# Hybrid token mixer: the input projection's three matmuls per weight tile become a 512-column and a 256-column one, with the halves added outside PSUM

## The chip, the cores and the metric

The kernel runs on 1 core of one Trainium2 chip. The metric is the device time of one execution in microseconds; the kernel before was timed in three runs, and their median is 1374.41 us (1373.37 to 1375.53). The engines of the core run side by side, each through its own list of instructions in a fixed order: TensorE (PE) does matmuls and loads their weights, VectorE (DVE) and ScalarE (ACT) do elementwise work, SyncE (SP) starts the weight transfers. PSUM is the memory that PE writes and that ACT and DVE read; everything else lies in SBUF.

## The reference

One layer on 256 tokens of width 2048. One input projection makes the inputs of three token mixers (Mamba-2 SSD, S5, RWKV-7), of their gates, and of three merge gates.

```python
proj = jnp.einsum('bsd,dc->bsc', x, w_in[l])          # 2048 -> 18592 columns
z_a, xbc, dt_raw, u_b, z_b, p_rkvz, p_w, p_a, p_gate = jnp.split(proj, offs, axis=-1)
y_a = mamba2_branch(z_a, xbc, dt_raw, ...)            # convolution over 4 tokens, SSD in chunks of 128
y_b = s5_branch(u_b, z_b, ...)                        # complex diagonal recurrence, GLU
y_c = rwkv7_branch(p_rkvz, p_w, p_a, ...)             # recurrence with 64x64 states, 16 heads
gates = jax.nn.sigmoid(p_gate.reshape(b, s, N_BRANCHES, d) + gate_b[l])
merged = (gates[:, :, 0] * (y_a @ w_branch_a[l]) + gates[:, :, 1] * (y_b @ w_branch_b[l])
          + gates[:, :, 2] * (y_c @ w_branch_c[l]))
x = layer_norm(DEEPNORM_ALPHA * x + merged @ w_out[l], ln_g[l], ln_b[l])
```

## The kernel before

Every large product is kept accurate by splitting both operands into a high and a low part of a rounded type (fp32r) and adding three products: high by high, high by low, low by high. The projection goes tile by tile, 128 output columns at a time, 145 tiles: 48 of the merge gates (`g0`, `g1`, `g2`), 32 of `x` (the input of the SSD convolution), 16 of `za`, 8 each of `z`, `v`, `u`, `r`, `k`, `zb`, and one `lora`. The name of a tile is the name of its PSUM tile: `ps_x4`, `ps_za5`.

For one tile `loadw` (L358) fetches 128 columns of weights as two half tiles; ACT makes their high part (L369) and DVE their low part (L371). Rings of four half tiles each (`raw`, `hi`, `lo`) let these run ahead of PE by two tiles. `proj` (L377) then issues, for each of 16 blocks of 128 input channels, three matmuls of 256 columns (the tokens): weights high by `xhi` (L381), weights high by `xlo` (L382), weights low by `xhi` (L383), 48 in a tile and 6960 in all, into one PSUM tile of a ring of three (tag `pj`). The weights are loaded into PE anew for each matmul. What uses a tile reads it straight from PSUM: the RWKV shift (`rwkv_shift`, ACT L439 and DVE L440) for `r`, `k`, `v`; the SSD convolution (`ssd_group`, one ACT pass L790 and three DVE passes L792) for `x`; a SiLU on ACT (L800) for `za`; a tanh (L512, L1189, L1201) for the gates.

Between these wide matmuls PE has small ones, 32 to 128 columns each, of the recurrences: the inverse of diagonal blocks (`py`, L647 to L655), the RWKV chunks (`ch`, L675 to L699: each chunk is a chain from PE to ACT or DVE and back), the SSD chunks (`st`, `y`, `cb`). Their order among the wide matmuls isn't written out: tables (`PROG` for the RWKV stage, `PROG2` for the rest) give the order of the stages and tiles, and a scheduler, with a model of the engines' times, lays all instructions out into one fixed list per engine; what stands under `high_priority` it draws forward. Engines wait for one another by semaphores. A new tile in a ring waits until the readers of the tile whose place it takes are done: `R` (the shifted `r`, ring of 2), `cv` (convolved tiles and gates of the SSD groups, ring of 11), `pj`.

After the projection tiles come the branch products (L1155 to L1157), the output product (L1257 to L1259, 512 columns) and the layer norm.

## Time and profile before

| | |
|---|---|
| time, median of 3 runs | 1374.41 us |
| span of the profiled execution | 1372.4 us |
| PE busy | 1353.5 us, 99% |
| DVE busy | 964.9 us, 70% |
| ACT busy | 829.1 us, 60% |
| share of the chain of work that ended last on PE | 97% |

Busy is time in which an engine ran something; the span runs from the first to the last recorded event of the profiled execution. The weight loads (PEld) overlap the matmuls. The duration printed for one matmul includes its passage through the array, and so is longer than the step from one matmul to the next: the steps are read from the starts.

### The profile page before, as it was taken

What the parts mean: (1) busy time and instruction counts of PE and PEld (TensorE: products, weight loads), DVE (VectorE), ACT (ScalarE), POOL (GpSimd) and SP (SyncE); (2) the same over time, 40 slices, a digit from 0 to 9 for tenths busy, and PEclk for the clock granted to TensorE, in tenths of its full rate; (3) what the DMA queues carried; (4) which work ended last, traced back from release to release, by engine and by line L of the source; (5) the groups of instructions that cost most, each with busy time, mean ns of one, the idle gap of its engine ahead of it and who ended that gap; (6) DMA issues with size and microseconds to landing.
All of it is one profiled execution on the core that took longest, in us unless ns stands there. A gap on an engine that the chain in (4) does not pass through costs nothing.

```text
span 1372.4 us, 28474 instructions
## 1 busy us (share of the span) xinstructions
PE 1353.5 (99%) x11436; PEld 1268.5 (92%) x11436; DVE 964.9 (70%) x1765; ACT 829.1 (60%) x1507; POOL 7.4 (1%) x54
## 2 busy tenths in 40 slices
PE   7999999999999999999999999999999999999996
PEld 7999989988999899899999999999999999999885
DVE  5658876455866765579999966799776665547755
ACT  5657565567555556887668877676645544444431
POOL 0000000000000000000000000000000000000000
PEclk9999999999999999999999999999999999999998
DMA  8545554433454345456555555555655556668751
GB/s 293 167 130 161 170 156 150 138 110 120 142 152 141 126 147 154 124 159 194 164 173 170 178 172 173 155 168 180 188 176 173 174 184 202 197 209 253 245 179 62
DMA packets 96661, 230.12 MB, mean 168 GB/s; under 512 B 26545, under 2 KB 41233, under 8 KB 96529
## 3 DMA queue, kind: packets, MB, share of 16 engines
q1 hardware_dynamic: 95936, 227.42, 53.9%
q8 instruction: 90, 1.47, 0.4%
q10 hardware_dynamic: 592, 0.89, 0.2%
q14 instruction: 43, 0.34, 0.1%
HBM read 224.00 MB, written 3.21 MB: 166 GB/s over the span
## 4 chain that ended last, share of the span: by engine, by line
PE 97%; ACT 1%; DMA 1%; DVE 1%; issue 0%; SPq 0%; DVEq 0%
PE ps_g L381 7%; PE ps_g L382 7%; PE ps_g L383 7%; PE ps_x L381 5%; PE ps_x L382 5%; PE ps_x L383 5%; PE br L1156 5%; PE br L1155 4%; PE br L1157 4%; PE po L1259 2%; PE po L1257 2%; PE po L1258 2%; PE ps_za L382 2%; PE ps_za L381 2%; PE ps_za L383 2%; PE ps_r L381 1%
## 5 line engine op out<-in xcount | busy, mean ns | idle before, releaser
L381 PE MATMUL ps_g<-xhi,hi_g 128*128 128x256 f32 x768 | 218.5, 284 | 0.0
L382 PE MATMUL ps_g<-xlo,hi_g 128*128 128x256 f32 x768 | 217.9, 284 | 0.0
L383 PE MATMUL ps_g<-xhi,lo_g 128*128 128x256 f32 x768 | 216.9, 282 | 0.0
L371 DVE TENSOR_TENSOR lo_g<-raw_g,hi_g 128x1024 fp32r<-128x1024 f32 x96 | 117.5, 1224 | 74.2 <-ACT hi_g L369 69.6
L369 ACT ACTIVATE hi_g<-raw_g 128x1024 fp32r<-128x1024 f32 x96 | 101.5, 1058 | 110.9 <-PE ps_g L382 81.8
L381 PE MATMUL ps_x<-xhi,hi_x 128*128 128x256 f32 x512 | 147.3, 288 | 0.0
L382 PE MATMUL ps_x<-xlo,hi_x 128*128 128x256 f32 x512 | 147.0, 287 | 0.0
L383 PE MATMUL ps_x<-xhi,lo_x 128*128 128x256 f32 x512 | 146.8, 287 | 0.0
L382 PEld LDWEIGHTS ps_g<-xlo,hi_g 128*128 128x128 f32 x768 | 144.6, 188 | 1.9 <-issue 0.8
L381 PEld LDWEIGHTS ps_g<-xhi,hi_g 128*128 128x128 f32 x768 | 144.6, 188 | 1.7
L383 PEld LDWEIGHTS ps_g<-xhi,lo_g 128*128 128x128 f32 x768 | 144.6, 188 | 0.9 <-issue 0.4
L369 ACT ACTIVATE hi_b<-raw_b 128x1024 fp32r<-128x1024 f32 x64 | 67.8, 1059 | 74.3 <-PE br L1156 42.9
L371 DVE TENSOR_TENSOR lo_x<-raw_x,hi_x 128x1024 fp32r<-128x1024 f32 x64 | 78.2, 1223 | 39.1 <-ACT hi_x L369 38.7
L381 PEld LDWEIGHTS ps_x<-xhi,hi_x 128*128 128x128 f32 x512 | 97.2, 190 | 2.3 <-issue 1.6
L382 PEld LDWEIGHTS ps_x<-xlo,hi_x 128*128 128x128 f32 x512 | 97.2, 190 | 2.1 <-issue 1.1
L383 PEld LDWEIGHTS ps_x<-xhi,lo_x 128*128 128x128 f32 x512 | 97.1, 190 | 1.6 <-issue 1.1
L369 ACT ACTIVATE hi_x<-raw_x 128x1024 fp32r<-128x1024 f32 x64 | 67.5, 1054 | 48.7 <-PE ps_x L382 25.1
L371 DVE TENSOR_TENSOR lo_b<-raw_b,hi_b 128x1024 fp32r<-128x1024 f32 x64 | 78.2, 1222 | 24.5 <-ACT hi_b L369 22.8
L382 PE MATMUL ps_za<-xlo,hi_za 128*128 128x256 f32 x256 | 73.1, 285 | 0.0
L381 PE MATMUL ps_za<-xhi,hi_za 128*128 128x256 f32 x256 | 73.0, 285 | 0.0
L383 PE MATMUL ps_za<-xhi,lo_za 128*128 128x256 f32 x256 | 72.6, 284 | 0.0
L1156 PE MATMUL br<-yh0l,hi_b 128*128 128x256 f32 x256 | 72.3, 283 | 0.0
(441 smaller groups left out, 4075.5 us busy)
## 6 DMA issues: line engine op xcount, KB each, us to landing
raw_g<-in_wt SPq DMA_DIRECT2D x96, 512.0 KB, 3.8
raw_x<-in_wt SPq DMA_DIRECT2D x64, 512.0 KB, 3.7
...
```

The costliest lines, as they stand in the source:

```text
L369: nc.scalar.activation(hi, raw, AF.Copy)
L371: nc.vector.tensor_tensor(lo, raw, hi.bitcast(F32), ALU.subtract)
L381: nc.tensor.matmul(ps, lhsT=hi.k(k), rhs=g.xhi[:, k, :], start=(k == 0), stop=False)
L382: nc.tensor.matmul(ps, lhsT=hi.k(k), rhs=g.xlo[:, k, :], start=False, stop=False)
L383: nc.tensor.matmul(ps, lhsT=lo.k(k), rhs=g.xhi[:, k, :], start=False, stop=(k == NK - 1))
L1155: nc.tensor.matmul(ps, lhsT=hi.k(k0 + k), rhs=h, start=(k == 0), stop=False)
L1156: nc.tensor.matmul(ps, lhsT=hi.k(k0 + k), rhs=l, start=False, stop=False)
L1157: nc.tensor.matmul(ps, lhsT=lo.k(k0 + k), rhs=h, start=False, stop=(k == n - 1))
L1257: nc.tensor.matmul(po, lhsT=m[0][:, t], rhs=hi.k512(k), start=f0, stop=False)
L1258: nc.tensor.matmul(po, lhsT=m[0][:, t], rhs=lo.k512(k), start=False, stop=False)
L1259: nc.tensor.matmul(po, lhsT=m[1][:, t], rhs=hi.k512(k), start=False, stop=l0)
```

## The change

`xhi` and `xlo` become the two halves of one tile `xx`, so that a weight tile's high part can be streamed against both as one matmul of 512 columns. The PSUM tile is twice as wide: its first half gathers high by high, its second half high by low and then, from a 256-column matmul, low by high. There are two matmuls for each block, 4640 in all, where there were three, and two loads of weights. At the end of a tile ACT copies the second half into SBUF and DVE adds the first half to it, both drawn forward by priority. What used PSUM before now reads that sum. The sum goes into a new ring of two (`pjs`) or, for `g2`, `za`, `zb` and the other gates, into the tile that the next step works on anyway. The ring `pj` keeps three buffers.

```diff
-    g.xhi = g.xf.tile([128, NK, T], F32R, name="xhi")
-    g.xlo = g.xf.tile([128, NK, T], F32R, name="xlo")
+    g.xx = g.xf.tile([128, NK, 2, T], F32R, name="xx")
+    g.xhi, g.xlo = g.xx[:, :, 0, :], g.xx[:, :, 1, :]
...
+        g.pjs = lambda nm: g.rp.tile([128, T], F32, nm, "pjs", 2)
...
+        g.pjs = lambda nm: kp.tile([128, T], F32, name=nm, tag="pjs", bufs=2)
...
-    def proj(n):
+    def proj(n, out=None):
         hi, lo = loadw(I["wt"][TIDX[n]], n, parts=4 if n in ("lora", "k0", "k1") else 1)
-        ps = g.pp.tile([128, T], F32, name="ps_" + n, tag="pj", bufs=3)
+        ps = g.pp.tile([128, 2, T], F32, name="ps_" + n, tag="pj", bufs=3)
         for k in range(NK):
-            nc.tensor.matmul(ps, lhsT=hi.k(k), rhs=g.xhi[:, k, :], start=(k == 0), stop=False)
-            nc.tensor.matmul(ps, lhsT=hi.k(k), rhs=g.xlo[:, k, :], start=False, stop=False)
-            nc.tensor.matmul(ps, lhsT=lo.k(k), rhs=g.xhi[:, k, :], start=False, stop=(k == NK - 1))
-        return ps
+            nc.tensor.matmul(ps, lhsT=hi.k(k), rhs=g.xx[:, k, :, :], start=(k == 0), stop=False)
+            nc.tensor.matmul(ps[:, 1, :], lhsT=lo.k(k), rhs=g.xhi[:, k, :], start=False, stop=(k == NK - 1))
+        with tc.high_priority():
+            s = g.pjs("pj_" + n) if out is None else out
+            nc.scalar.activation(s, ps[:, 1, :], AF.Copy)
+            nc.vector.tensor_tensor(s, ps[:, 0, :], s, ALU.add)
+        return s
...
-        ps = g.proj(f"za{2 * gr + q}")
         z = g.cv(f"zs{q}_{gr}")
+        ps = g.proj(f"za{2 * gr + q}", z)
         with tc.high_priority():
             nc.scalar.activation(z, ps, AF.Silu)
```

The scheduler lays the instructions out anew. The wide tiles keep their order on PE; the small matmuls move against them. Two places matter below. In the kernel after, the two wide matmuls are L384 (512 columns) and L385 (256), and the copy and the add are L388 (ACT) and L389 (DVE); other lines after `proj` stand six further down.

**From `za4` to `za5` (SSD stage).** On PE before, the small matmuls `y0` (SSD group 0), `ch6`, `ch7` (RWKV chunks of heads 6 and 7) stood in groups inside projection tiles, here inside `ps_x4`:

```order
L381 MATMUL ps_x4_7170<-xhi_69,hi_x4_0_7160 128x256
L852 MATMUL y0_6645<-csb1_0_6604,xdt0_6619 64x128 x2
L856 MATMUL y0_6645<-Cd0_6630,ST0_6628 64x128 x2
L852 MATMUL y0_6645<-csb0_0_6602,xdt0_6619 64x128 x2
L852 MATMUL y0_6645<-csb1_0_6604,xdt0_6619 64x128
L680 MATMUL ch7_1_5360<-X7_1_5365,TTf3_3764 64x64 x2
L680 MATMUL ch6_2_5382<-X6_2_5387,TTf3_3764 64x64 x2
L852 MATMUL y0_6645<-csb1_0_6604,xdt0_6619 64x128
L856 MATMUL y0_6645<-Cd0_6630,ST0_6628 64x128 x2
L382 MATMUL ps_x4_7170<-xlo_70,hi_x4_0_7160 128x256
```

Their neighbours on PE now begin where `ps_za4` ends:

```order
L385 MATMUL ps_za4_6469<-xx_69,lo_za4_1_6467 128x256
L384 MATMUL ps_za4_6469<-xx_69,hi_za4_1_6465 128x512
L385 MATMUL ps_za4_6469<-xx_69,lo_za4_1_6467 128x256
L661 MATMUL py3_0_4542<-TTf3_3302,Yl3_0_4543 32x32 x4
L686 MATMUL ch6_0_4655<-X6_0_4658,TTf3_3302 64x64 x2
L681 MATMUL ch7_0_4671<-SVA7_3660,XS7_3642 64x64 x2
L653 MATMUL py3_1_4574<-cst_167,TTf3_3302 32x32 x4
L693 MATMUL ch6_0_4655<-SVA6_3458,bkT6_3459 64x64 x2
L657 MATMUL py3_1_4574<-Yl3_1_4575,Aoff3_3301 32x32 x4
L703 MATMUL ch6_0_4655<-MTr6_3483,SVA6_3458 64x64 x2
```

and end where `ps_za5` begins, 45 rows (87 matmuls) later, with no wide matmul among them:

```order
L681 MATMUL ch7_2_4753<-SVA7_3660,XS7_3642 64x64 x2
L858 MATMUL y0_5807<-csb1_0_5766,xdt0_5781 64x128 x2
L862 MATMUL y0_5807<-Cd0_5792,ST0_5790 64x128 x2
L858 MATMUL y0_5807<-csb0_0_5764,xdt0_5781 64x128 x2
L858 MATMUL y0_5807<-csb1_0_5766,xdt0_5781 64x128 x2
L862 MATMUL y0_5807<-Cd0_5792,ST0_5790 64x128 x2
L681 MATMUL ch6_3_4775<-SVA6_3458,XS6_3440 64x64 x2
L686 MATMUL ch7_2_4753<-X7_2_4758,TTf3_3302 64x64 x2
L384 MATMUL ps_za5_6518<-xx_69,hi_za5_0_6508 128x512
L385 MATMUL ps_za5_6518<-xx_69,lo_za5_0_6510 128x256
```

So the small matmuls of some 23 groups now form one block between two tiles. `ps_za5` takes the PSUM buffer of `ps_x18`, and so waits until that has been copied and added. On ACT before, the convolution of `x4` (`xs0_2`) stood ahead of the chunk's next copies, and read PSUM:

```order
L677 ACTIVATE X7_2_5409<-ch7_2_5404 128x64
L369 ACTIVATE hi_x18_1_7300<-raw_x18_1_7298 128x1024
L790 ACTIVATE xs0_2_7219<-ps_x4_7170,par_166 128x256
L677 ACTIVATE X6_3_5431<-ch6_3_5426 128x64
L683 ACTIVATE SVA7_4174<-ch7_2_5404 64x64 x2
L817 ACTIVATE BT1_7085<-cb1_7081 128x128
L683 ACTIVATE SVA6_3946<-ch6_3_5426 64x64 x2
```

On ACT now it stands behind the decay factors (`csb`, `Cd`) of SSD groups 0 and 1, and the copy of `ps_x18` nine rows behind it:

```order
L689 ACTIVATE SVA7_3660<-ch7_1_4709 64x64 x2
L796 ACTIVATE xs0_2_6288<-pj_x4_6285,par_165 128x256
L689 ACTIVATE SVA6_3458<-ch6_2_4731 64x64 x2
L851 ACTIVATE csb1_0_5766<-csb1_0_5766 128x512
L851 ACTIVATE csb0_1_6159<-csb0_1_6159 128x512
L677 ACTIVATE SVA7_3660<-S7_1_4722 64x64 x2
L699 ACTIVATE SW7_2_4767<-S7_1_4722,W47_3636 128x64
L677 ACTIVATE SVA6_3458<-S6_2_4744 64x64 x2
L706 ACTIVATE XS7_3642<-ch7_1_4709 128x64
L706 ACTIVATE XS6_3440<-ch6_2_4731 128x64
L388 ACTIVATE pj_x18_6393<-ps_x18_6360 128x256
L799 ACT_TABLE_LOAD
```

The copy `pj_x18` writes the `pjs` slot that `pj_x4` held, which `xs0_2` reads; `xs0_2` writes a `cv` slot that DVE's product of `Cd0` with the tile `C_0` frees.

**From `u3` to `g2_13` (RWKV stage).** On PE before, the block inverse of batch 1 (`py1`) began inside `ps_r6`:

```order
L383 MATMUL ps_k7_3700<-xhi_69,lo_k7_1_3698 128x256
L715 MATMUL rlb0_2193<-rhl_229,selT_227 128x256
L715 MATMUL rlb1_2198<-rhl_229,selT_227 128x256
L647 MATMUL py1_0_2282<-cst_168,TTf1_1044 32x32 x4
L381 MATMUL ps_r6_3780<-xhi_69,hi_r6_0_3770 128x256
L382 MATMUL ps_r6_3780<-xlo_70,hi_r6_0_3770 128x256
```

On PE now its matmuls follow the end of `ps_u3`:

```order
L384 MATMUL ps_u3_3722<-xx_69,hi_u3_1_3718 128x512
L385 MATMUL ps_u3_3722<-xx_69,lo_u3_1_3720 128x256
L721 MATMUL rlb0_1944<-rhl_228,selT_226 128x256
L721 MATMUL rlb1_1949<-rhl_228,selT_226 128x256
L653 MATMUL py1_0_2033<-cst_167,TTf1_926 32x32 x4
L653 MATMUL py1_1_2065<-cst_167,TTf1_926 32x32 x4
L653 MATMUL py1_0_2033<-cst_167,TTf1_926 32x32 x4
L681 MATMUL ch2_0_2669<-SVA2_1082,XS2_1064 64x64 x2
L657 MATMUL py1_0_2033<-Yl1_0_2034,Aoff1_925 32x32 x8
```

and go on to the start of `ps_g2_13`, 19 rows (63 matmuls) after `ps_u3`:

```order
L591 MATMUL pv4_2419<-cst_167,V4_2364 64x64 x4
L693 MATMUL ch2_0_2669<-SVA2_1082,bkT2_1083 64x64 x2
L657 MATMUL py1_1_2065<-Yl1_1_2066,Aoff1_925 32x32 x4
L597 MATMUL pt4_1_2436<-cst_167,BK4_2408 128x64 x4
L384 MATMUL ps_g2_13_3771<-xx_69,hi_g2_13_0_3761 128x512
L385 MATMUL ps_g2_13_3771<-xx_69,lo_g2_13_0_3763 128x256
```

Between them stand the shift's partners of head 4 (`bon4`, `pv4`, `pt4`). `ps_g2_13` takes the PSUM buffer of `ps_r7`, whose copy waits for the `pjs` slot of `pj_r6`; the shift that reads that slot writes an `R` slot that `bon4` is the last to read.

## Rows read from the trace of the kernel before

**Rows 1.** The page: span, busy time of the engines, chain that ended last.

```profile
span 1372.4 us, 28474 instructions
...
PE 1353.5 (99%) x11436; PEld 1268.5 (92%) x11436; DVE 964.9 (70%) x1765; ACT 829.1 (60%) x1507; POOL 7.4 (1%) x54
...
PE 97%; ACT 1%; DMA 1%; DVE 1%; issue 0%; SPq 0%; DVEq 0%
```

**Rows 2.** The waits of PE, whole span: us in total, times, longest.

```profile
PE ps_dt L320 <- ACT wd L315: 7.0, 1, 7.0
PE ps_lora L383 <- DVE lo_lora L371: 0.4, 1, 0.4
```

**Rows 3.** PE in a projection tile, in order of time: start, duration (us).

```profile
1150.01 0.28 PE L382 MATMUL ps_g<-xlo,hi_g 128*128 128x256 f32 x1
...
1156.07 0.28 PE L382 MATMUL ps_g<-xlo,hi_g 128*128 128x256 f32 x1
```

**Rows 4.** PE in the output product, in order of time, 512 columns.

```profile
1290.60 0.39 PE L1259 MATMUL po<-hi_wo,mgl 128*128 128x512 f32 x1
...
1299.89 0.39 PE L1259 MATMUL po<-hi_wo,mgl 128*128 128x512 f32 x1
```

**Rows 5.** PE in two stretches: busy us (matmuls), PEclk, DMA share, GB/s.

```profile
519.00:563.00 44.00, 43.94 (x402) 1.00 0.49 154
270.00:289.00 19.00, 19.00 (x194) 1.00 0.45 140
```

**Rows 6.** The same two stretches, the wide matmuls of line L383 alone.

```profile
519.00:563.00 44.00, 24.09 (x85) 1.00 0.49 154
270.00:289.00 19.00, 9.37 (x33) 1.00 0.45 140
```

**Rows 7.** One turn from PE to ACT, in order of time.

```profile
519.77 0.22 PE L680 MATMUL ch<-X,TTf 64*64 64x64 f32 x1
...
520.02 0.45 ACT L683 ACTIVATE SVA<-ch 64x64 f32<-64x64 f32 x2 [0.27 <-PE ch L680]
```

**Rows 8.** ACT, groups by line and shape: busy us, mean ns, idle before.

```profile
L369 ACT ACTIVATE hi_x<-raw_x 128x1024 fp32r<-128x1024 f32 x64 | 67.5, 1054 | 48.7 <-PE ps_x L382 25.1 <-PE ps_za L382 13.0 <-PE br L1156 5.1
...
L844 ACT ACTIVATE csb<-csb,csT 128x128 f32<-128x128 f32 x64 | 20.3, 391 | 0.2
...
L838 ACT ACT_TABLE_LOAD x7 | 9.0, 1283 | 0.1
...
L677 ACT ACTIVATE X<-ch 128x64 f32<-128x64 f32 x32 | 6.6, 220 | 0.9 <-PE ch L675 0.3
...
L800 ACT ACTIVATE zs<-ps_za 128x256 f32<-128x256 f32 x16 | 5.9, 370 | 0.1
```

**Rows 9.** ACT among the SSD factors, in order of time.

```profile
649.51 0.63 ACT L838 ACTIVATE Cd<-csb 128x512 f32<-128x512 f32 x1
650.17 1.28 ACT L844 ACTIVATE csb<-csb,csT 128x128 f32<-128x128 f32 x4
651.49 0.63 ACT L845 ACTIVATE csb<-csb 128x512 f32<-128x512 f32 x1
```

**Rows 10.** DVE, groups by line and shape.

```profile
L371 DVE TENSOR_TENSOR lo_x<-raw_x,hi_x 128x1024 fp32r<-128x1024 f32 x64 | 78.2, 1223 | 39.1 <-ACT hi_x L369 38.7
...
L792 DVE SCALAR_TENSOR_TENSOR xs<-ps_x,par,xs 128x254 f32<-128x254 f32 x16 | 7.7, 479 | 0.3
...
L1217 DVE TENSOR_TENSOR sgb<-br,sgb 128x256 f32<-128x256 f32 x16 | 6.8, 425 | 6.3 <-PE br L1157 6.3
```

**Rows 11.** PE after a run of small matmuls, in order of time.

```profile
461.86 0.34 PE L383 MATMUL ps_x<-xhi,lo_x 128*128 128x256 f32 x1
...
462.00 0.41 PE L381 MATMUL ps_x<-xhi,hi_x 128*128 128x256 f32 x1
...
465.20 0.35 PE L381 MATMUL ps_x<-xhi,hi_x 128*128 128x256 f32 x1
```

**Rows 12.** All engines by stretch: PE, PEld, DVE, ACT, POOL busy us (instructions), PEclk, DMA share, GB/s.

```profile
400.00:500.00 100.00, 100.00 (x874) 90.91 (x873) 68.28 (x139) 55.74 (x120) 0.46 (x3) 0.98 0.44 136
500.00:600.00 100.00, 99.94 (x895) 90.09 (x894) 52.92 (x84) 73.25 (x160) 0.31 (x2) 1.00 0.46 138
600.00:700.00 100.00, 100.00 (x885) 97.13 (x885) 95.72 (x249) 70.76 (x139) 0.53 (x5) 1.00 0.60 181
700.00:800.00 100.00, 100.00 (x920) 95.29 (x920) 91.36 (x191) 80.94 (x157) 0.73 (x7) 1.00 0.57 170
```

More of the change, by code (lines that the diff above doesn't have):

```diff
@@ L394 @@
 class RwkvPools:
-    EARLY = {"K", "sq", "R", "V", "tA", "tB", "tC", "tD", "wlr", "wlh", "wll", "EE", "BK", "Aa", "xlh", "xll"}
+    EARLY = {"K", "sq", "R", "V", "tA", "tB", "tC", "tD", "wlr", "wlh", "wll", "EE", "BK", "Aa", "xlh", "xll", "pjs"}
     MIDDLE = {"AT", "TT", "Pm", "Yl", "XS0", "SVA0", "bkT0", "MTr0", "bon0", "Aoff0", "TTf0"}
@@ L509, in gate_c @@
 def gate_c(g, j):
-    ps = g.proj(f"g2_{j}")
+    ps = g.proj(f"g2_{j}", g.acc[j])
     with g.tc.high_priority():
@@ L1160, in s5_zb @@
 def s5_zb(g, j):
-    pz = g.proj(f"zb{j}")
+    g.zb[j] = g.ycr(f"zb{j}")
+    pz = g.proj(f"zb{j}", g.zb[j])
     with g.tc.high_priority():
-        g.zb[j] = g.ycr(f"zb{j}")
         g.nc.scalar.activation(g.zb[j], pz, AF.Silu)
@@ L1185, in gate_b @@
 def gate_b(g, j):
-    pg = g.proj(f"g1_{j}")
     g.sgb[j] = g.yar(f"sgb{j}")
+    pg = g.proj(f"g1_{j}", g.sgb[j])
     with g.tc.high_priority():
@@ L1197, in branch @@
     if br == 0:
-        pg = g.proj(f"g0_{j}")
         sg = g.fp.tile([128, T], F32, name=f"sg{j}", tag="sg", bufs=1)
+        pg = g.proj(f"g0_{j}", sg)
         with g.tc.high_priority():
```

## The prediction

> **What bounds the kernel now.** I read the page first: PE is busy for 1353.5 us of a span of 1372.4, and 97% of the chain that ended last is PE's [rows 1]. Then the waits of PE: 7.0 us for the first weights, 0.4 us at `lora`, nothing after that [rows 2]. So PE is late everywhere and early nowhere, and the end moves with whatever is taken from or put into PE's own list. Last the steps between the starts of its matmuls, since the printed durations hold the passage through the array: in a projection tile 51 steps of 256 columns last 1156.07 - 1150.01 = 6.06 us, 0.1188 each [rows 3]; in the output product 41 steps of 512 columns last 9.29 us, 0.2266 each [rows 4]. ACT and DVE stay below PE, but not far below it between 600 and 800 us, where DVE is busy for 95.7 and 91.4 of 100 us and ACT for 70.8 and 80.9 [rows 12].
>
> **The matmuls.** A block of a tile costs 3 x 0.1188 = 0.3565 us now and 0.2266 + 0.1188 = 0.3454 after, 0.0111 less. There are 145 x 16 = 2320 blocks: **-25.7 us**, all of it on PE's path. The two rows say the same in another way: 256 columns more cost 0.1078, so 0.0111 of every step doesn't grow with the columns, and one such part goes. The 512-column steps are read from other operands; if each end of the two readings is off by 0.0015 the gain is 22 to 29 us. Against this speaks the Trainium skill, page "TensorE: Matmul & The Clock Gate", section "Wait — 56ns, not 53.3ns?": a fixed cost of some 2.5 ns for each matmul at the full clock. By it the 2320 matmuls removed would be worth 2320 x 0.0025 = 5.8 us, and the sum 20 us higher. The rows differ from it, since 0.1188 and 0.2266 leave 11 ns; I go by the rows.
>
> **Copies and adds.** 145 copies on ACT and 145 adds on DVE come in. The nearest rows are a SiLU of the same shape from PSUM, 0.37 us [rows 8], and a product with a PSUM operand, 0.425 [rows 10]: 54 us on ACT, 62 on DVE, beside PE. Reading SBUF instead gives nothing back that I would count. Over the span there is room. In 600 to 800 us there is hardly any on DVE: some 28 tiles bring 28 x 0.425 = 12 us, PE needs 28 x 16 x 0.0111 = 5 less, and DVE's idle time there is 4.3 + 8.6 = 13 us. That would make DVE late by up to 4 us if none of its work moved; it can be drawn ahead by two tiles of weights, so I take 0 and keep 4 for the range. Weights arrive as before: DMA at 0.46 to 0.60 of the engines' time [rows 12].
>
> What costs time is the new order. A tile's PSUM buffer is now freed by copy and add, these wait for a `pjs` slot, and the slot for the convolution or shift two tiles back. In PE's list there are two places where small matmuls that wait on one another form one block between two wide tiles; before, they stood in groups inside wide tiles, so that PE had work during each turn through ACT or DVE.
>
> **First block, `u3` to `g2_13`.** From the end of `u3`: the high part `hi_g2_14_1` needs the place of `hi_u3_1` (1.05 us [rows 8]), its low part follows on DVE (1.22 [rows 10]) and stands ahead of the add that `rlb0` needs (0.4): 2.7 us. From there the chain is DVE's: seven passes of 0.42 to 0.48 us, four on heads 0 and 1's outputs and three longer ones on head 4 (4.5 us in all); `bon4` on PE with a turn, 0.6; then on ACT the shift of `r6`, three copies and the copy of `r7`, and two DVE passes of 0.45 between (3 us). Together 10.8 us from `u3` to `g2_13`. Before, the same 63 matmuls were 63 of the 194 - 3 x 33 = 95 small ones in 270 to 289 us, which cost 19.0 - 99 x 0.1188 = 7.2 us [rows 5, 6]; by count that is 4.8, and as they lay in smaller groups than the mean I take 5.6. Net **+5.2 us** (2 to 8).
>
> **Second block, `za4` to `za5`.** PE may not start `za5` before ACT's copy of `ps_x18`, at the end of 47 rows of ACT. First `hi_x6_1`, 1.05 us after `za4`'s end. Then 18 chunk copies between 0.22 and 0.5 us (26 instructions, 6.3 us), with some 12 turns in which ACT waits for PE: a copy starts 0.25 us after its matmul [rows 7], 3.0 us. Then 27 rows with few turns: one table load of 1.28 us [rows 8], twelve passes of `csb` at 20.3 / 64 = 0.32 [rows 8, 9], four exponentials of 0.63 [rows 9], the convolution, and some fifteen copies of 0.22 to 0.37 (12 us in all, 10.8 where their records overlap). The add of `x18`, 0.43. Sum 21.6 to 22.8; I take 21.6, since some turns lie under other copies. Before, these 87 matmuls were part of the 402 - 255 = 147 small ones in 519 to 563 us, which cost 43.9 - 255 x 0.1188 = 13.6 us [rows 5, 6]: by count 8.0, and as they filled 23 groups of about four I take 10.1. Net **+11.5 us** (7 to 17).
>
> **The clock.** PE at half its clock takes 0.2133 us for 256 columns: 15 steps in 3.20 us at 462 us, behind 3 us of small matmuls [rows 11], with PEclk at 0.98 in that stretch of 100 us [rows 12]. The steps are those of the lower level, 1.2 GHz, against 2.4 elsewhere. Both blocks keep PE from wide matmuls for longer than that, so I expect the same return behind each: 15 x (0.2133 - 0.1188) = 1.4 us, **+3 us** for two (0 to 6).
>
> **ACT behind the second block.** ACT leaves it with nothing done ahead. From there to the high part of the branch weights `b2_4` its rows sum to 69 us by the means of [rows 8] and to some 63 where overlapping records are taken off; PE's wide and small matmuls to that point sum to about 62. I take **+2.5 us** (0 to 12).
>
> Sum: -25.7 + 5.2 + 11.5 + 3 + 2.5 = **-3.5 us**. The profiled span of 1372.4 becomes 1368.9; it lies 2.0 below the median of the runs, 1374.4, with the start and end of an execution around it that the change doesn't touch, so the time is 1374.4 - 3.5 = 1370.9, rounded to **1371 us**. Fewer interruptions of wide work elsewhere (the list has some six groups less) may give 1 or 2 more, which I leave in the range.
>
> **Rivals.** (a) *The waits are hidden.* If PE's blocks take no longer than the groups did, what stays is the matmuls: 1374.4 - 25.7 = 1349 us, or up to 1361 where only the second block waits. For it: PE waits nowhere now, and 407 us of DVE's span and 543 of ACT's are idle [rows 1]. Against it: the two blocks stand in the lists, and no wide matmul can pass them.
> (b) *ACT becomes the bound from `za5` on.* The place is `za6` to the branch tiles `b2_0` to `b2_4`, where the new copies, five more table loads and the block's leftovers meet. If ACT's rows cost their means, 69 us, and the low part follows 1.2 us later, PE waits some 12 us instead of 2.5 and falls to the lower clock again (+1.5 to 3): -3.5 + 9.5 + 3 = +9, **1383 us**. It decides from the point where ACT is more than 9 us late there. For it: ACT is the fullest in 700 to 800 us [rows 12] and its order is fixed. Against it: in the trace the records of ACT overlap.
> (c) *The change doesn't do what it says.* If a 512-column step in a projection tile takes as long as two of 256 (0.2376), nothing is saved, and the waits stay: -3.5 + 25.7 = +22, **1397 us**. Against it: such a step is 0.2266 in the trace [rows 4]. With the gain that the 2.5 ns of the Trainium skill ("TensorE: Matmul & The Clock Gate", same section) leave it would be 1391 us; the same row speaks against that.
>
> **How the numbers follow.** The forecast has 0.52 (1363 to 1379: 0.30 of it faster, 0.18 the same, 0.04 slower), (a) 0.19, all faster, (b) 0.24 (0.03 the same, 0.21 slower), (c) 0.05, slower. Within 0.2%, 2.7 us, is about what a measurement can't tell from no change. Faster 0.49, same 0.21, slower 0.30. The range leaves out (c), the upper end of (b) and the lower end of (a): 1352 to 1387. The forecast's own range is 1363 to 1379.
>
> **What would show it.** Steps of 0.345 us for a pair L384, L385; other than that, (c). Waits of PE at `ps_za5` and `ps_g2_13`, with windows of about 22 and 11 us between the wide tiles and PEclk below 1 behind them; a window below 14 us at `za5` speaks for (a). Waits of PE for `hi` or `lo` of `za6` to `b2_4` above 9 us: (b). The forecast is wrong if PE waits at a third place that its list doesn't show as a block, or if DVE holds it up in 600 to 800 us.

## The result, and the profile after

The changed kernel takes 1386.75 us (median of 4 runs, 1384.92 to 1387.78) where the kernel before takes 1374.97 beside it: a ratio of 1.0085, 95% interval 1.0071 to 1.0099, 11.8 us slower. The wide range of the prediction, 1352 to 1387, just holds it. The forecast's own range, 1363 to 1379, does not, and the direction is the other one.

The page of the kernel after: span, busy time, the granted clock in 40 slices, and the chain that ended last.

```profile
span 1384.9 us, 24116 instructions
...
PE 1348.6 (97%) x9116; PEld 1149.5 (83%) x9116; DVE 1009.9 (73%) x1910; ACT 882.7 (64%) x1657; POOL 7.5 (1%) x54
...
PEclk9999999989999999889999999999999999999998
...
PE 90%; ACT 5%; DVE 2%; DMA 1%; issue 1%; SPq 0%; DVEq 0%; ACTq 0%
```

PE has 2320 matmuls less than in [rows 1], yet its busy time falls by 4.9 us only. Its share of the chain falls from 97% to 90%; ACT and DVE have 5% and 2% of it, where they had 1% each. The granted clock falls below nine tenths in the slices of the two blocks and in the last.

The waits of PE in the kernel after, largest first: total us, times, longest. [Rows 2] had two.

```profile
PE ps_dt L322 <- ACT wd L317: 6.7, 1, 6.7
PE rlb L721 <- DVE rhl L478: 2.8, 1, 2.8
PE ch L693 <- ACT SVA L689: 2.4, 3, 1.3
PE st L839 <- DVE xdec L837: 1.6, 1, 1.6
PE br L1161 <- DVE acc L1221: 1.3, 1, 1.3
PE br L1162 <- DVE yh2l L395: 1.1, 1, 1.1
```

No wait is at `ps_za5` or `ps_g2_13`, where the prediction put them. PE now waits in front of small matmuls inside the two blocks, and later twice for DVE in the branch products (`br`). By the time it comes to the wide tile behind a block, the tile's buffer is free: by 1.6 us at `g2_13`, by 2.1 at `za5`.

**The pair.** PE in the late gate tiles, in order of time: start, duration (us). These answer [rows 3].

```profile
1204.22 0.39 PE L384 MATMUL ps_g<-xx,hi_g 128*128 128x512 f32 x1
1204.45 0.28 PE L385 MATMUL ps_g<-xx,lo_g 128*128 128x256 f32 x1
...
1248.80 0.39 PE L384 MATMUL ps_g<-xx,hi_g 128*128 128x512 f32 x1
```

From the first to the last of these starts lie 44.58 us and 127 pairs without a break: 0.3510 us a pair. Three matmuls of 256 columns took 0.3565, so a block gains 0.0055 and not the 0.0111 of the forecast.

**The blocks.** Two stretches of the kernel after, from the start of the last wide matmul ahead of a block to the start of the first behind it: us, busy time of PE (matmuls), granted clock, DMA share, GB/s.

```profile
295.27:311.17 15.90, 12.00 (x118) 0.58 0.20 67
571.92:597.52 25.60, 18.86 (x176) 0.61 0.26 75
```

PE in the first block and behind it, in order of time; in brackets what it waited for. The first row is an earlier `bon`, for comparison.

```profile
58.87 0.59 PE L579 MATMUL bon<-R,cst 128*128 128x256 f32 x2
...
298.38 0.77 PE L721 MATMUL rlb<-rhl,selT 64*128 64x256 f32 x2 [2.83 <-DVE rhl L478]
...
304.97 1.22 PE L579 MATMUL bon<-R,cst 128*128 128x256 f32 x2
...
311.17 0.79 PE L384 MATMUL ps_g<-xx,hi_g 128*128 128x512 f32 x1
311.77 0.41 PE L385 MATMUL ps_g<-xx,lo_g 128*128 128x256 f32 x1
...
314.91 0.28 PE L385 MATMUL ps_g<-xx,lo_g 128*128 128x256 f32 x1
```

The block begins with the wait for `rhl` that was forecast (2.7; 2.83 here). Then PE is busy nearly throughout, at a granted clock of 0.58 over the stretch, near the lower of its levels (1.2 of 2.4 GHz): one `bon` matmul, which leaves two records in the trace, takes 1.22 us there and 0.59 in the first row. The pairs behind the block start at the lower level too, and reach the higher at 314.91. The second block, in the same way:

```profile
584.45 1.22 PE L839 MATMUL st<-xdec,BT 128*128 128x256 f32 x2 [1.57 <-DVE xdec L837]
...
589.79 0.48 PE L693 MATMUL ch<-SVA,bkT 128*64 128x64 f32 x4 [1.29 <-ACT SVA L689]
...
594.58 0.38 ACT L388 ACTIVATE pj_x<-ps_x 128x256 f32<-128x256 f32 x1
594.99 0.42 DVE L389 TENSOR_TENSOR pj_x<-ps_x,pj_x 128x256 f32<-128x256 f32 x1 [2.23 <-ACT pj_x L388]
...
597.52 0.77 PE L384 MATMUL ps_za<-xx,hi_za 128*128 128x512 f32 x1
```

The copy and add of `x18` are done at 595.41; PE has its own small matmuls until 597.52.

**Where the time went.** I put each step from one start to the next, over the whole trace, to one of three kinds: a wide matmul's usual step, up to 1.25 times its normal length; what a wide step takes beyond that; a group of small matmuls between two wide ones, less one wide step. The sums run to the start of the last wide matmul. What is called normal is a choice; with other choices the terms shift by up to 0.7 us against one another.

| us | before | after | difference |
|---|---|---|---|
| projection, usual steps | 833.1 | 821.2 | -11.9 |
| projection, what is over in long steps | 18.4 | 15.0 | -3.4 |
| branch and output products, usual steps | 293.0 | 293.5 | +0.5 |
| the same, what is over in long steps | 1.5 | 5.6 | +4.1 |
| groups of small matmuls (252; 217) | 199.9 | 223.1 | +23.2 |
| to the first projection matmul | 14.9 | 15.4 | +0.5 |
| sum | 1360.8 | 1373.8 | +13.0 |

The two blocks are 15.78 and 25.48 us of the groups after. What follows asks two things: why the 512-column step is long, and what put 23 us into the groups.

### The profile page after: what moved, and what is told of

It reads as the page before. It is cut to its first block, busy times and chain, and to the rows that moved or that the text cites. A ratio compares the mean times of both kernels' runs of the same rounds, so it can differ in the third digit from the quotient of the medians.

```text
span 1384.9 us, 24116 instructions
## 1 busy us (share of the span) xinstructions
PE 1348.6 (97%) x9116; PEld 1149.5 (83%) x9116; DVE 1009.9 (73%) x1910; ACT 882.7 (64%) x1657; POOL 7.5 (1%) x54
## 4 chain that ended last, share of the span: by engine, by line
PE 90%; ACT 5%; DVE 2%; DMA 1%; issue 1%; SPq 0%; DVEq 0%; ACTq 0%
PE ps_g L384 13%; PE ps_x L384 8%; PE ps_g L385 7%; PE ps_x L385 4%; PE br L1161 4%; PE br L1162 4%; PE br L1163 4%; PE ps_za L384 4%; PE ps_r L384 2%; PE ps_z L384 2%; PE ps_k L384 2%; PE ps_v L384 2%; PE ps_u L384 2%; PE po L1265 2%; PE po L1264 2%; PE po L1263 2%
## 5 line engine op out<-in xcount | busy, mean ns | idle before, releaser
L384 PE MATMUL ps_g<-xx,hi_g 128*128 128x512 f32 x768 | 277.9, 400 | 0.5 <-ACT hi_g L371 0.5
L385 PE MATMUL ps_g<-xx,lo_g 128*128 128x256 f32 x768 | 219.3, 286 | 0.7 <-DVE lo_g L373 0.7
L384 PE MATMUL ps_x<-xx,hi_x 128*128 128x512 f32 x512 | 183.9, 397 | 0.0
L384 PEld LDWEIGHTS ps_g<-xx,hi_g 128*128 128x128 f32 x768 | 145.0, 189 | 34.2 <-issue 0.8
L385 PE MATMUL ps_x<-xx,lo_x 128*128 128x256 f32 x512 | 147.9, 289 | 0.0
L385 PEld LDWEIGHTS ps_g<-xx,lo_g 128*128 128x128 f32 x768 | 145.2, 189 | 2.7 <-DVE lo_g L373 1.3
L384 PEld LDWEIGHTS ps_x<-xx,hi_x 128*128 128x128 f32 x512 | 96.2, 188 | 21.1 <-issue 0.6
L385 PEld LDWEIGHTS ps_x<-xx,lo_x 128*128 128x128 f32 x512 | 96.3, 188 | 2.7 <-issue 1.2
L384 PE MATMUL ps_za<-xx,hi_za 128*128 128x512 f32 x256 | 92.1, 398 | 0.0
L385 PE MATMUL ps_za<-xx,lo_za 128*128 128x256 f32 x256 | 73.6, 288 | 0.0
L384 PEld LDWEIGHTS ps_za<-xx,hi_za 128*128 128x128 f32 x256 | 48.2, 188 | 11.1 <-issue 0.7
L373 DVE TENSOR_TENSOR lo_wo<-raw_wo,hi_wo 128x1024 fp32r<-128x1024 f32 x32 | 38.5, 1223 | 23.2 <-ACT hi_wo L371 21.8
```

The source lines that it names most:

```text
L373: nc.vector.tensor_tensor(lo, raw, hi.bitcast(F32), ALU.subtract)
L384: nc.tensor.matmul(ps, lhsT=hi.k(k), rhs=g.xx[:, k, :, :], start=(k == 0), stop=False)
L385: nc.tensor.matmul(ps[:, 1, :], lhsT=lo.k(k), rhs=g.xhi[:, k, :], start=False, stop=(k == NK - 1))
```

## The experiments

Unless said, the difference shown is to the kernel after; "pair" is the 512- and the 256-column matmul of a block. In each, lines move a little, so that a wide matmul has another line number.

**Is it the alternation, or the 512-column matmul itself?** Late tiles of `g1` in other forms, in one kernel:

```diff
+        if n in ("g1_9", "g1_13"):
+            for k in range(NK):
+                mm(ps, lhsT=hi.k(k), rhs=g.xx[:, k, :, :], start=(k == 0), stop=False)
+            for k in range(NK):
+                mm(ps[:, 1, :], lhsT=lo.k(k), rhs=g.xhi[:, k, :], start=False, stop=(k == NK - 1))
+        elif n in ("g1_10", "g1_14"):
...
+                mm(ps[:, 0, :], lhsT=lo.k(k), rhs=g.xhi[:, k, :], start=False, stop=(k == NK - 1))
+        elif n in ("g1_3", "g1_15"):
...
+                mm(ps, lhsT=lo.k(k), rhs=g.xx[:, k, :, :], start=False, stop=(k == NK - 1))
```

The first form has all 16 of 512 columns ahead of all 16 of 256; the second adds the third product to the other half; the third streams `xx` against the low weights too. Two more have two of 512 and two of 256 in turn, and three of 256 columns.

> The changed kernel, with the 16 matmul pairs of ten of the tiles g1 issued in five other forms, two tiles each, late in the program where nothing waits. In the changed kernel's trace a run of 127 pairs takes 0.3510 us a pair where I had forecast 0.3454. Theory A: the 512-column matmul costs its 0.2266 only when its neighbours have 512 columns too, and each change between 512 and 256 columns costs some 3 ns. Then all 16 wide matmuls ahead of all 16 narrow ones give 0.3454 a block, two and two 0.348, and two 512-column matmuls 0.453. Theory B: a 512-column matmul into the two-part tile takes 0.2315 whatever stands beside it. Then all ahead gives 0.351 and two of 512 columns 0.463. Theory C: the narrow matmul, which adds to the half that the wide one wrote last, waits for it. Then adding to the first half instead gives 0.3454, and B's and A's forms only change where the half is left alone for longer. Three matmuls of 256 columns in the two-part tile: 0.3564 by all.

PE in that kernel, in order of time; x16 is 16 matmuls in a row:

```profile
1206.76 3.88 PE L385 MATMUL ps_g<-xx,hi_g 128*128 128x512 f32 x16
1210.48 2.09 PE L387 MATMUL ps_g<-xx,lo_g 128*128 128x256 f32 x16
1212.40 3.88 PE L385 MATMUL ps_g<-xx,hi_g 128*128 128x512 f32 x16
1216.13 2.06 PE L387 MATMUL ps_g<-xx,lo_g 128*128 128x256 f32 x16
1218.03 0.39 PE L390 MATMUL ps_g<-xx,hi_g 128*128 128x512 f32 x1
```

Sixteen steps of 512 columns last 3.72 and 3.73 us, 0.233 each, sixteen of 256 last 1.92 and 1.90, 0.119 each. So the 512-column step is 0.233 among its like, with no alternation, against 0.2266 in [rows 4]. Two and two gave 0.3495 a pair (32 pairs in 11.18 us), the other half of the PSUM tile 0.3513, two of 512 in turn 0.2324 each, against 0.3510 for the pair as it is: neither the neighbour nor the half of the tile makes the long step. Three of 256 columns took 0.3555 a block in one tile and 0.3600 in the other.

**Which operand, and does it grow with the columns?** In late `g1` tiles (their output isn't the projection's) the held and the streamed operand are exchanged for weights or for `x`, and `x` is streamed with fewer columns:

```diff
+        if n == "g1_9":
...
+                    mm(ps, lhsT=(hi, lo)[q].k(k), rhs=g.xx[:, k, :, :], start=(k + q == 0), stop=(k == NK - 1 and q == 1))
+        elif n == "g1_13":
...
+                    mm(ps, lhsT=(hi, lo)[q].k(k), rhs=(hi, lo)[q].t[k // 8][:, 4 * (k % 2):4 * (k % 2) + 4, :], start=(k + q == 0), stop=(k == NK - 1 and q == 1))
+        elif n == "g1_10":
...
+                    mm(ps, lhsT=g.xx[:, k, 0, 128 * q:128 * q + 128], rhs=(hi, lo)[q].t[k // 8][:, 4 * (k % 2):4 * (k % 2) + 4, :], start=(k + q == 0), stop=(k == NK - 1 and q == 1))
```

A fourth form has `x` on both sides; three more stream the first 256, 384 and 448 columns of `x`.

> The changed kernel; in seven of the late tiles g1 the 32 matmuls are replaced by others that leave their results of no use, and only the steps are read. In one tile the weights' high and low parts are held and both halves of x streamed (512 columns, as measured 0.2323 a step); in one the same weights are held and 512 columns of weights streamed; in one x is held and weights streamed, as in the output product (0.2266); in one x is held and x streamed. Three more stream 256, 384 and 448 columns of x. Theory B1: what is streamed decides: x gives 0.232, weights 0.227 whatever is held. B2: what is held decides: weights held 0.232, x held 0.227. B3: the place in the program decides (what ACT, DVE and the transfers do beside it): all four 0.232. The steps of 256, 384 and 448 columns tell whether the excess grows with the columns (0.1188, 0.1755, 0.204) or comes in one step at the end (0.1188, 0.172, 0.199).

The first matmul of three forms, and the last of the third; PE in order of time, 32 matmuls to a form:

```profile
1203.48 0.39 PE L386 MATMUL ps_g<-xx,hi_g 128*128 128x512 f32 x1
...
1210.93 0.39 PE L390 MATMUL ps_g<-hi_g 128*128 128x512 f32 x1
...
1218.21 0.40 PE L394 MATMUL ps_g<-hi_g,xx 128*128 128x512 f32 x1
...
1225.42 0.39 PE L394 MATMUL ps_g<-lo_g,xx 128*128 128x512 f32 x1
```

Weights held and `x` streamed: 7.45 us for 32 steps, 0.233. Weights by weights: 7.28 us, 0.2275. `x` held and weights streamed: 7.21 us for 31 steps, 0.2326. `x` by `x`: 0.2284. So it hangs on the pair of operands, and neither the held nor the streamed one alone explains it; none of the three theories fits all four. With `x` streamed the step is 0.1187 for 256 columns, 0.176 for 384, 0.2039 for 448 and 0.2326 for 512. Twice 0.1187 less 0.2326 leaves 0.0048 that doesn't grow with the columns, for this operand in this place; times 2320 that is 11.1 us, and the trace gave 11.9.

**Does its place in memory matter?** The same, with `x` streamed from 96 columns (384 bytes) on in its row, with one set of weights held twice, and with the activations of the branch products held:

```diff
+        elif n == "g1_13":
...
+                    mm(ps, lhsT=(hi, lo)[q].k(k), rhs=g.xx.rearrange("p k a t -> p (k a t)")[:, 512 * min(k, 14) + 96:512 * min(k, 14) + 608], start=(k + q == 0), stop=(k == NK - 1 and q == 1))
+        elif n == "g1_10":
...
+                    mm(ps, lhsT=hi.k(k), rhs=g.xx[:, k, :, :], start=(k + q == 0), stop=(k == NK - 1 and q == 1))
...
+        elif n == "g1_3":
...
+                    mm(ps, lhsT=g.acts[1][k // 2][q][:, 128 * (k % 2):128 * (k % 2) + 128], rhs=g.xx[:, k, :, :], start=(k + q == 0), stop=(k == NK - 1 and q == 1))
```

> The changed kernel, again with the matmuls of seven late tiles g1 replaced (their results are of no use), 32 of 512 columns each, to see on which operands the step of 0.2324 hangs. So far: weights held and x streamed 0.2324, x held and weights streamed 0.2324, both weights 0.2272, both x 0.228, output product 0.2266. Now: weights held, x streamed; the same with the streamed columns shifted by 96; high weights held in both matmuls of a pair, x streamed; branch activations held, weights streamed; branch activations held, x streamed; both weights; high weights held in both, weights streamed. Theory G: it hangs on the pair of places in SBUF that are read at once, x and the weight rings: then only the pairs of weights and x take 0.232, shifted or not, and activations with either 0.227. Theory H: it hangs on the load of the held part: with the same weights held twice 0.227 or less. If the shifted columns take 0.227, it is their alignment.

The start of the first form, and the first and last matmul of the shifted one:

```profile
1203.38 0.39 PE L387 MATMUL ps_g<-xx,hi_g 128*128 128x512 f32 x1
...
1210.83 0.39 PE L391 MATMUL ps_g<-xx,hi_g 128*128 128x512 f32 x1
...
1217.88 0.39 PE L391 MATMUL ps_g<-xx,lo_g 128*128 128x512 f32 x1
```

31 shifted steps last 7.05 us, 0.2274, where `x` from its place took 0.233. With weights or branch activations held, `x` from its place took 0.233 and the weights 0.2265 to 0.2271. So the place of what is streamed has a part in it, and the natural next step was to move `x` in the whole kernel (the last of the experiments).

**Copies and adds without the wide matmul.** Three matmuls of 256 columns for every block but the first of a tile; tiles, rings, copies and adds of the kernel after:

```diff
+        for k in range(1, NK):
+            mm(ps[:, 0, :], lhsT=hi.k(k), rhs=g.xhi[:, k, :], start=False, stop=False)
+            mm(ps[:, 1, :], lhsT=hi.k(k), rhs=g.xlo[:, k, :], start=False, stop=False)
+            mm(ps[:, 1, :], lhsT=lo.k(k), rhs=g.xhi[:, k, :], start=False, stop=(k == NK - 1))
```

> Only the second part of the change: the two-part PSUM tile, the copy on ACT and the add on DVE, but three 256-column matmuls a block as before (a pair of 512 and 256 in the first of 16 blocks). PE's list then has no block of small matmuls between two tiles. My theory now, that copies and adds are hidden and that the loss lies in the two blocks and their order: 1375 us, within 3 us of the kernel before. Rival, that the 54 us of copies and 62 us of adds hold PE up by themselves: 1385 us or more.

1384.41 us against 1375.07, ratio 1.0062 (1.0041 to 1.0084). Its largest waits of PE behind the first tiles:

```profile
PE y L865 <- ACT ST L844: 3.8, 1, 3.8
...
PE ssps L469 <- ACT ksq L494: 0.7, 1, 0.7
PE y L861 <- DVE csb L855: 0.5, 2, 0.3
```

The scheduler makes neither of the two blocks here, though the ring of two and the copies are the same. The groups still cost 10.5 us more than before (210.4; the traced execution is the slowest of four, 1387.04). So copies and adds, with the order they bring, cost 9 us by themselves, and they don't make the blocks. ACT ahead of the longest wait, which ends at 656.52:

```profile
651.32 1.28 ACT L809 ACT_TABLE_LOAD   x1
...
653.89 0.36 ACT L391 ACTIVATE zs<-ps_za 128x256 f32<-128x256 f32 x1
654.27 1.28 ACT L854 ACT_TABLE_LOAD   x1
...
656.10 0.37 ACT L844 ACTIVATE ST<-st 128x256 f32<-128x256 f32 x1
```

A copy (L391) stands in ACT's list ahead of `ST`, but so do two loads of ACT's function tables, 1.28 us each where the copy takes 0.36: in this wait the order around the copies counts, and not only their own time.

**The wide matmul without copies and adds.** Users read the first half of the PSUM tile, so the second half's products are left out of the result:

```diff
-        with tc.high_priority():
-            s = g.pjs("pj_" + n) if out is None else out
-            nc.scalar.activation(s, ps[:, 1, :], AF.Copy)
-            nc.vector.tensor_tensor(s, ps[:, 0, :], s, ALU.add)
-        return s
+        return ps[:, 0, :]
```

> Only the first part of the change: 512 and 256 columns a block, and no copy and no add, the tiles are read from PSUM. This leaves out the second half of each tile's sum (what goes over the low parts), so that no wait of the changed kernel's copies is left. The list has again two blocks of small matmuls, of 56 between x18 and x26 and of 50 between r7 and v7. Theory: the matmuls give back 2320 x 0.0054 = 12.5 us, and the blocks cost in proportion to their size, 106 of 150 matmuls and 23 us, some 16 us: 1374 to 1380 us. Rival, that it is the ring of the copies that makes the blocks wait: 1362 us, with windows at the blocks no longer than their matmuls.

1390.89 us, ratio 1.0104 (1.0080 to 1.0129): no faster than with the copies. Its list has two blocks of its own, behind `x18` and behind `r7`, of 18.0 and 16.4 us, with these waits:

```profile
PE y L858 <- ACT ST L837: 5.5, 2, 5.3
PE rlb L717 <- DVE rhl L474: 5.0, 1, 5.0
PE y L854 <- DVE csb L848: 2.2, 1, 2.2
```

The wide steps are 822.4, near the 821.2 of the kernel after, the groups 225.8. Blocks come, then, with the 512-column form and the order that the scheduler makes of it; they need neither the `pjs` ring nor the copies.

**The order alone.** Two kernels with all of before, in which one entry of the tables is moved, so that small matmuls fall elsewhere:

```diff
-PROG = ("... z4 g2_5 u6 z7 F3 u3 ...
+PROG = ("... z4 g2_5 u6 F3 z7 u3 ...
```

> The kernel before with one entry of its table of the RWKV stage moved: the front of batch 3 (F3) one place ahead of the tile z7. No instruction comes in or goes. Theory D: the order of the kernel before is one in which PE never waits, and the order that the scheduler gives to a slightly different program is in general not, so that the order alone costs some us: 1378 to 1385 us, with waits of small matmuls of 5 us or more in all. Rival: the order costs nothing unless blocks form, and copies and adds are what costs: 1373 to 1377 us and no waits.

```diff
-PROG2 = ("dt ch S0 S1 S2 S3 c0 c1 ...
+PROG2 = ("dt ch S0 S1 S2 c0 S3 c1 ...
```

> The kernel before with one entry of its second table moved: the branch tile c0 one place ahead of the SSD group 3. No instruction comes in or goes; PE's list differs in the SSD stage, where ACT and DVE are fullest. Theory D: 1377 to 1384 us, waits of small matmuls for ACT or DVE in the SSD stage. Rival, that the order costs nothing: 1373 to 1377 us.

1377.56 us, ratio 1.0023 (1.0013 to 1.0033), and 1375.32, 1.0008 (0.9997 to 1.0018). These two orders cost 3 us and nothing that is clear of noise, less than the theory wanted. By themselves they reach neither the 9 us of the copies nor the 23 of the groups; two small moves don't show that no order could.

**Copies and adds that nobody reads.** The three matmuls and the readers of before (with `x` in the one tile `xx`), in which 105 tiles are also copied and added into the ring, beside their usual readers:

```diff
+            s = g.pjs("pj_" + n)
+            nc.scalar.activation(s, ps, AF.Copy)
+            nc.vector.tensor_tensor(s, ps, s, ALU.add)
```

> The kernel before, with a copy on ACT and an add on DVE for each of the 105 projection tiles up to the SSD stage that nothing reads: the tiles are used from PSUM as before, and only the work of copies and adds comes in (and the PSUM buffer is held until they are done). With copies and adds used, as in the changed kernel, and 256-column matmuls, the time was 9.3 us above that of the kernel before, 6.7 us of it waits of PE that the kernel before doesn't have. Theory E: it is the work, 39 us on ACT and 45 on DVE at engines that are 80 to 95% busy in the SSD stage, that makes small matmuls wait: 1381 to 1385 us, with waits for ACT's ST or DVE's csb. Theory F: it is the longer way from a tile's last matmul to its use, copy, add and then the shift or convolution: 1375 to 1378 us. A change of order alone cost 0.6 and 2.8 us.

1397.56 us, ratio 1.0170 (1.0153 to 1.0187). Its waits of PE, and its engines in 700 to 800 us (columns as in [rows 12]):

```profile
PE ps_za L383 <- DVE B L799: 3.7, 2, 2.7
...
PE ps_za L383 <- DVE xs L799: 2.2, 1, 2.2
PE y L863 <- ACT ST L842: 2.1, 3, 1.0
```

```profile
700.00:800.00 100.00, 92.88 (x853) 88.80 (x852) 91.08 (x203) 74.89 (x153) 0.84 (x8) 0.97 0.51 153
```

PE is busy for 92.88 us in the stretch where it was for 100.00 in [rows 12]; it waits for PSUM buffers that DVE frees late, and for the chunk's turns. That the load of copies and adds in the SSD stage can cost PE time is shown by this; the size can't be carried over, since here a buffer is held by the copy and by its old reader too. The other theory of the expectation, the longer way to a tile's use, can't account for this run, whose users read PSUM as before; for the changed kernel it isn't excluded.

**How the price grows with the tiles that are changed.** The wide form, copy and add for some tiles alone, the old three matmuls for the others. Gate tiles, `za` and `zb` (72):

```diff
+        if n[0] != "g" and n[0:2] not in ("za", "zb"):
+            pt = g.pp.tile([128, T], F32, name="ps_" + n, tag="pj", bufs=3)
+            for k in range(NK):
+                mm(pt, lhsT=hi.k(k), rhs=g.xhi[:, k, :], start=(k == 0), stop=False)
+                mm(pt, lhsT=hi.k(k), rhs=g.xlo[:, k, :], start=False, stop=False)
+                mm(pt, lhsT=lo.k(k), rhs=g.xhi[:, k, :], start=False, stop=(k == NK - 1))
+            return pt
```

> The change in the 72 tiles of the gates alone (g0, g1, g2, za, zb); the tiles x, r, k, v, z, u and lora keep three matmuls and are read from PSUM. No small matmul waits on these 72 tiles, and the list has no block between two tiles. Theory: 72 x 16 x 0.0054 = 6.2 us less, 1368 us. Rival, that copies and adds cost PE something wherever they stand: 1375 us or more.

`g0` and `g1` alone (32), all of which lie behind the recurrences:

```diff
+        if n[0:2] not in ("g0", "g1"):
...
```

> The change in the 32 tiles g0 and g1 alone, which lie late in the program; the order of PE's list up to the SSD stage stays that of the kernel before. Theory, that the wide matmul gives 0.0052 us a block and nothing waits on the gates' copies: 32 x 16 x 0.0052 = 2.7 us less, 1372.4 us. By theory D a wait or two where the list differs, in the stage of branch a, could eat it: 1373 to 1377. Rival, that copies and adds cost PE 0.07 us each, as 9.3 us over 145 in the run with copies only: 1377 us.

`g0`, `g1`, `g2` (48), the same way:

> The change in the 48 tiles g0, g1 and g2 alone. With g0 and g1 the time was 3 us below the kernel before; with g2, za and zb too it was 5.4 above, though 1152 blocks were cheaper by 6 us. This tells where that went. If g2 (in the RWKV stage) costs nothing: 48 x 16 x 0.0052 = 4 us below, 1371 us. If every copied tile before the SSD stage's end costs some 0.2 us: 1375 us. If za or zb are what costs, as in theory E, g2 shows no waits.

`g0`, `g1`, `zb` (40):

> The change in the 40 tiles g0, g1 and zb. zb lies in the last part of the SSD stage, where DVE is 86 to 96% busy. If zb costs nothing: 40 x 16 x 0.0052 = 3.3 us below the kernel before, 1371.5 us. If theory E holds: 1373 to 1376 us, with waits of small matmuls at 700 to 1000 us.

Steps and groups summed as above, against the kernel before (833.1 and 199.9):

| tiles changed | time | ratio | usual projection steps | groups |
|---|---|---|---|---|
| `g0 g1` (32) | 1371.69 | 0.9978 (0.9968 to 0.9987) | -3.1 | -0.4 |
| `g0 g1 zb` (40) | 1372.05 | 0.9979 (0.9968 to 0.9990) | -3.3 | +0.3 |
| `g0 g1 g2` (48) | 1373.96 | 1.0000 (0.9991 to 1.0009) | -3.4 | +4.5 |
| `g`, `za`, `zb` (72) | 1380.17 | 1.0039 (1.0025 to 1.0054) | -5.5 | +9.2 |
| all (145) | 1386.75 | 1.0085 (1.0071 to 1.0099) | -11.9 | +23.2 |

The waits of PE with the 32 late tiles are those of the start:

```profile
PE ps_dt L322 <- ACT wd L317: 6.9, 1, 6.9
PE ps_lora L387 <- DVE lo_lora L373: 0.5, 1, 0.5
PE ps_dt L323 <- DVE xx L314: 0.3, 1, 0.3
```

The gain follows the number of blocks: 32 x 16 x 0.0055 = 2.8 us, 3.1 measured. The price begins with the first tiles that lie among the recurrences, `g2` in the RWKV stage and `za` in the SSD stage, and there it is larger than the gain: with `g2` the kernel is back at the time before. (The traced execution with `g2` is the slowest of ten, 1377.40, so its +4.5 is high.) With the late tiles alone the kernel is faster than both, by 0.2% against before.

**Moving `x`.** In each kernel all of `x` lies 384 or 128 bytes lower in SBUF, the order of all engines unchanged. The pools `ap` and `sp`, which the kernel opens on the same side behind `x`, move with it; they hold tiles of the branch products and of S5. The weight rings stay where they were. For the kernel after, the kernel before, and the version with 40 late tiles:

```diff
-    g.xx = g.xf.tile([128, NK, 2, T], F32R, name="xx")
+    g.xx = g.xf.tile([128, NK * 2 * T + 96], F32R, name="xx")[:, 0:NK * 2 * T].rearrange("p (k a t) -> p k a t", k=NK, a=2)
```

(`+ 96` for 384 bytes, `+ 32` for 128; in the kernel before the same at `xlo`, which moves `xhi` and `xlo`.)

> The changed kernel with the tile xx 384 bytes lower in SBUF (96 unused columns behind it), so that its rows begin where the weight tiles' rows do, and nothing else: the order of every engine's list is the same. In the last look the streamed columns shifted by 96 took 0.2274 a step instead of 0.2326. Theory G', that the place of x in SBUF makes its 512-column step slow: 0.0050 x 2320 = 11.6 us off the wide matmuls, 1375 us. Rival, that the shift in the probe mattered only by the columns it left out, or that the new place is as slow: 1386 us, pairs at 0.351.

> The change in the 40 tiles g0, g1 and zb, with x 384 bytes lower; the order is that of the run with these 40 tiles (1372.0 us, 2.5 us below the kernel before). Theory G': 640 blocks at 0.0050 us less, 3.2 us below that run, 1369 us, and more if the 256-column step of the other 105 tiles gets shorter too (by up to 0.0013, as the branch products between 0.1175 and 0.1200 show: 6.6 us more, 1362). Rival: 1372 us.

> The kernel before with xhi and xlo 384 bytes lower in SBUF, and nothing else. If the place of x makes the 256-column step long too: from 0.1187 to 0.1175, 6960 x 0.0012 = 8 us, 1366 us. If only steps of more than 256 columns depend on it: 1374.5 us, which then says that the change's gain lies in the wide step at the right place.

> The kernel before with xhi and xlo 128 bytes lower in SBUF instead of 384, and nothing else. 384 bytes made its 256-column step 0.1198 instead of 0.1187 and the time 8 us longer, with the same order. If the place matters by its offset within 512 bytes, then 128 bytes lower is the offset (352 of 512) at which the shifted columns took 0.2274: the step gets shorter, 0.1175 and 1367 us. If every place other than the one before is worse, or the offset counts within 2048 bytes: 1375 to 1383 us.

> The changed kernel with xx 128 bytes lower, and nothing else. By the first of the two, pairs of 0.346 and 1375 us; else pairs of 0.351 or more and 1386 to 1391 us.

> The change in the 40 tiles g0, g1 and zb (1372.0 us), with x 128 bytes lower. By the first, 1361 to 1369 us; else 1372 to 1377 us.

| | time | ratio to the kernel before |
|---|---|---|
| after, 384 bytes | 1390.60 | 1.0116 (1.0099 to 1.0133) |
| after, 128 bytes | 1390.53 | 1.0123 (1.0107 to 1.0138) |
| before, 384 bytes | 1383.03 | 1.0062 (1.0047 to 1.0077) |
| before, 128 bytes | 1381.49 | 1.0055 (1.0038 to 1.0071) |
| 40 late tiles, 384 bytes | 1377.31 | 1.0022 (1.0012 to 1.0032) |
| 40 late tiles, 128 bytes | 1377.23 | 1.0024 (1.0015 to 1.0034) |

All are slower than the same kernel with `x` unmoved, and not one gave the short 512-column step. The kernel before with `x` 384 bytes lower, PE in a projection tile (compare [rows 3]):

```profile
1150.03 0.28 PE L382 MATMUL ps_g<-xlo,hi_g 128*128 128x256 f32 x1
...
1156.15 0.28 PE L382 MATMUL ps_g<-xlo,hi_g 128*128 128x256 f32 x1
```

51 steps in 6.12 us, 0.1200, against 0.1188: with the same order and no new wait of more than 0.2 us, the projection steps alone make some 7 us (833.1 to 839.7 in the sums), and the branch steps some 2. In the kernel after with `x` moved the 512-column step is 0.2341 and the one of 256 behind it 0.1170, 0.3511 together as before, but the branch steps are 0.1198. So `x` stood in a good place for 256 columns before; which places are good, and why, stays open. No kernel was run with `x` higher, the direction in which the shifted form took 0.2274.

## Why the prediction was wrong

**The matmuls: the step that failed.** The forecast took the 512-column step of a projection tile from the output product, 0.2266 [rows 4], and allowed for 0.0015 at each end. In the projection it is 0.231 to 0.233, so 25.7 us became 11.9. That is 13.8 of the 16.5 us between the sum forecast (-3.5) and the trace (+13.0), and without it there would have been no loss: with 25.7 the sum would have been -0.8. "The same shape" was not enough for a price: the other operands there, or their place, were 0.006 us off, half of the 0.011 that was to be gained. What doesn't grow with the columns, read between two sizes of the *same* operand in the same place, is 0.0048 us (2 x 0.1187 - 0.2326) and not 0.0111. The Trainium skill, page "TensorE: Matmul & The Clock Gate", section "Wait — 56ns, not 53.3ns?", gives some 2.5 ns; by an estimate from that figure the gain would have been 5.8 us. The trace, at 4.8 ns, lies between, nearer to the page than to my row; I was wrong to set the page's warning aside whole rather than let it lower the gain.

**The blocks: the places right, the cause and the sizes partly not.** Both are where the order showed them. Together they cost 16.4 us net where 16.7 was forecast, but by errors that cancel, which is luck. Each lasts longer (15.8 and 25.5 for 10.8 and 21.6): the forecast followed ACT's and DVE's chains, while PE itself was busy for 12.00 and 18.86 us there, at a granted clock of 0.58 and 0.61. And the small matmuls had cost more before than I counted: the trace has two records for most of these matmuls, and 63 and 87 in the list are 116 and 174 records (118 and 176 in the windows above, each with two wide ones), so that of the 95 and 147 small records of [rows 5, 6] I gave them about half their share. By records, which is how those rows count, 116 / 95 x 7.2 = 8.8 and 174 / 147 x 13.6 = 16.1 us were their price before, and 7.0 and 9.4 are net. That `za5` waits for the copy of `x18` was wrong: the buffer was free 2.1 us ahead of PE, and the form without copies has blocks of the same kind.

**Copies and adds: not free.** They were costed at 0, with 4 in the range. The form without the wide matmul lost 9.3 us. What the profile did show was room in the sum of busy time; what that sum doesn't show is what stands in a fixed list ahead of a turn that PE waits for (`ST`, `csb`, `ksq` above). The new order also brings ACT 80 table loads where it had 75, and 15 instead of 8 between 600 and 700 us; seven more at 1.28 us are 9.0 of the 11.1 us by which ACT is busier there. The forecast had named more table loads only in its rival (b). In 600 to 700 us PE is busy for 96.64 where it was for 100.00 in [rows 12]:

```profile
600.00:700.00 100.00, 96.64 (x702) 85.65 (x701) 82.96 (x213) 81.84 (x154) 0.37 (x3) 1.00 0.47 148
700.00:800.00 100.00, 99.05 (x727) 85.31 (x726) 93.67 (x205) 78.16 (x162) 0.74 (x7) 1.00 0.55 176
```

Of the 23.2 us of the groups the two blocks are 16.4; the other 6.8 lie outside them. That they are of this kind is likely from the run with copies alone, but not shown tile by tile, and how much of it is the load and how much the order can't be split: each experiment that takes one away has another order.

**The clock.** +3 was forecast; the pairs behind the blocks lose 1.75 us (311.17 to 314.91, less five pairs of 0.351 and a step of 0.231) and 0.4 us (one pair, 597.52 to 598.25, less 0.351). The larger effect, the small matmuls *inside* the block at the lower level, was left out of the sum.

**ACT behind the second block.** +2.5 was forecast for ACT's backlog up to the branch tiles; the long steps of the branch products grew by 4.1. The two longest waits there are for DVE (`yh2l`, 1.1; `acc`, 1.3). Ahead of the second, which ends at 666.11, DVE itself had waited for ACT:

```profile
662.54 0.19 DVE L958 SCALAR_TENSOR_TENSOR s5t<-s5t 128x32 f32<-128x32 f32 x1 [1.69 <-ACT s5t L950]
```

The chain that ended last runs through ACT from 649 to 663 us here, then through DVE to `acc`. So the place was right, and for this wait ACT's lateness too, by way of DVE and not of the weights; for `yh2l`, where DVE had been busy since 650.26, it is not shown.

**The rivals.** (a) falls: the waits aren't hidden. (b) came nearest to the time, 1383, without being the cause: no wait of 9 us stands at `za6` to `b2_4`. (c) holds by half: the step isn't 0.2376, but the saving is less than half of what the row promised; "some of the gain, and the waits stay" would have given -3.5 + 13.8 = +10, and I had priced only its extreme.
